# Two heads' float32 products of a gated recurrence take turns in the two row halves of the TensorE array

## The chip, the cores and the metric

The kernel runs on one core of one Trainium2 chip. The metric is the device time of one execution in microseconds (us); a smaller time is better. A kernel is timed in several executions, and the median is compared.

## What is computed

The reference is one layer of a diffusion backbone for 640 tokens of 1024 channels: 128 context tokens and 512 latent ones. One input projection feeds three branches (attention, a gated linear recurrence in both directions, a Fourier mixing); each is gated, and one output projection closes the layer. The change lies in the recurrence, cut here to one direction:

```python
def step(s, inp):                        # one chunk of 64 positions, 4 heads of 64 x 64
    qc, kc, vc, gc = inp
    G = jnp.cumsum(gc, axis=2)           # gc: log of the forget gates
    diff = G[:, :, :, None, :] - G[:, :, None, :, :]
    decay = jnp.exp(jnp.where(causal[:, :, None], diff, -jnp.inf))
    attn = jnp.einsum('bhtd,bhsd,bhtsd->bhts', qc, kc, decay)
    o = jnp.einsum('bhtd,bhde->bhte', qc * jnp.exp(G), s) + jnp.einsum('bhts,bhse->bhte', attn, vc)
    ...
    s_new = jnp.exp(G_last[:, :, 0, :])[..., None] * s + jnp.einsum(
        'bhsd,bhse->bhde', kc * jnp.exp(G_last - G), vc)
    return s_new, o
...
return o_f + flip(o_b), jnp.stack([s_f, s_b], axis=1)
```

## The kernel before, in words

**Tiles.** Channels lie on the 128 partitions, and the 640 tokens are five tiles of 128: tile 0 is the context, tiles 1 to 4 are latent. The recurrence has four heads of 64 channels, worked on as two pairs: pair p has one head on partitions 0 to 63 (`hh` = 0) and the other on 64 to 127 (`hh` = 1), so that a product of one head alone uses one row half of the TensorE array.

**Levels.** The products of queries and keys under their decays (`attn` above, both directions in one matrix) are built by `recurrence(p)` in seven levels, with block lengths 1, 2, 4 ... 64 (`LEVELS`, line 23). At a level, ScalarE copies the halves of the decayed queries and keys into `QB` and `KB` (lines 449 to 452); VectorE and GpSimd multiply the queries and keys by their gates for the next level (455 to 458), and VectorE multiplies the gates of neighbours (463, 464). Then `level` (432 to 439) forms, for each head, five float32 products of 64 x 128 by 64 x 128, one a token tile: four into one PSUM bank, the fifth (`i` = 4) into another. VectorE copies out of the bank those positions that belong to this level (`copy_predicated` with the mask of the level, line 439) into `AL` (four tiles of both heads, 128 x 512 each head) and `AC` (the fifth, 128 x 128 each). The seven masks and the diagonal (476, 477) cover every position once. The order is: head 0, four tiles; head 1, four tiles; head 0, last tile; head 1, last tile. The vector work of a level does not read the products of the level before it; the two meet only in the banks and the buffers.

**After the levels** keys are transposed by token, the states before each tile are formed (`kt`, `pst`, `sall`), and outputs are products of `AL`, `AC` with the values and of the decayed queries with the states.

**PSUM.** Five banks have the tag `b` (`WB["pb"]`), three the tag `f`. `PB()` takes the next of the five; the projections that run beside the recurrence accumulate in `f` banks.

**What sets the order.** Each part of the work is a generator; the class `Order` merges them, earlier streams first, by the estimates in `LAT` and by `od.now`, which `mm` (111 to 114) advances. The recurrences and the attention come ahead of `fill()`, which delivers the input projections one block after another (`zb0 qr0 zb1 qr1 ir0 P0 P1 ga0 ...`, P being the value, query and key blocks of an attention pair). The framework then schedules all of it again by a timeline of its own (`schedule_with_timeline_sim`; `IN_ORDER` is off), so the final order on each engine is fixed when the kernel is built, and each engine works through its list in order.

**Projections** are sums of three products of float32r parts (`mm3`): "W, hT" rows of 128 x 320 or, for `ir0`, 128 x 256. They are the work with which TensorE fills the time in which the levels' operands are made.

Of the kernel before, what the change touches and what calls it, by code (L numbers as in the profile page):

```python
# [17 lines left out]
P = 128  # L18
# [21 lines left out]
class Order:  # L40
    """Merges streams of statements into one: each is a generator that yields after a piece of TensorE work, with the
    time in us that its next piece has to wait for other engines, or the name of an event; earlier streams go first."""
# [30 lines left out]
def mixer_kernel(ctx: ExitStack, tc: tile.TileContext, A, O):  # L73
# [37 lines left out]
    def mm(out, lhsT, rhs, start=True, stop=True):  # L111
        n, m = rhs.free_size(), lhsT.free_size()
        od.now += 1e-3 * (n * 0.4167 * 4 if rhs.dtype == F32 else max(n * 0.4167, m * 0.83)) + 2e-3
        te.matmul(out, lhsT, rhs, start=start, stop=stop)  # L114
# [28 lines left out]
    # lower bounds of the forget gates: softmax and running sum over depth (one layer)  # L143
# [9 lines left out]
    def rsqrt_mean(ss, n):  # L153
        """ss -> 1/sqrt(ss/n + eps), in place."""
# [23 lines left out]
    def load_w(src, lo_eng=None, shape=(KT, P), tags=("raw", "hi", "lo")):  # L178
        """1024 weights a partition, in two parts"""
        return split_w(load_raw(src, tags[0], shape), lo_eng, shape, tags[1:])  # L180

    def load(t, src):
        """loads that follow the weights issued so far"""
# [3 lines left out]
    def mod_cols(out, w):  # L187
        """[4, 128]: rows 0,1 = c_hi (w_hi + w_lo), rows 2,3 = c_lo (w_hi + w_lo)."""
# [12 lines left out]
    def mm3(out, w, k, u, first, last):  # L201
        """out += w[:, k].T @ h[k][:, half u], in three passes over the parts."""
# [92 lines left out]
    def block(name, use, lo_eng=gp):  # L295
        """128 columns of the projection; use(z, u) gets one half of the tokens, z = [128 channels, 320 tokens] in PSUM."""
# [30 lines left out]
    def twice_silu(out, z):  # L327
        """2 silu(z) = z (1 + tanh(z / 2)): tanh is in the tables of exp and of the sigmoid"""
# [10 lines left out]
    def by_token(src):  # L339
        """[128 channels, 640 tokens] -> PSUM [128 tokens, token tile, 128 channels], the first four tiles and the last."""  # L340
# [5 lines left out]
    def token_blocks(name, use, tokens, lo_eng=gp):  # L346
        """256 columns of the projection by token; use(z, i0, n) gets token tiles i0 .. i0 + n - 1, z = [128 tokens, n, 256
        channels] in PSUM. tokens(t, i): tile i of the tokens."""
# [28 lines left out]
    # the mixed channels: a gate times its branch, put together by the later of the two  # L377
    mx, branch = [None] * 8, [None] * 8

    def mixed(j, gate=None, result=None):  # L380
        """result(out, gate): writes their product"""
# [30 lines left out]
    def recurrence(p):  # L412
# [9 lines left out]
        # [positions within the tile, head, tile, positions]: 4 latent tiles, and the context  # L422
# [6 lines left out]
        def level(KB, QB, mask):  # L429
            mk = late["masks"][:, mask, :].unsqueeze(1)  # L430
            for i0, i1 in ((0, 4), (4, 5)):
                for hh in range(2):
                    pa = PB()
                    w = (i1 - i0) * P
                    for i in range(i0, i1):
                        mm(pa[:, (i - i0) * P:(i - i0 + 1) * P], KB[RS[hh], i * P:(i + 1) * P],
                           QB[RS[hh], i * P:(i + 1) * P])
                    out = AL[:, hh] if i0 == 0 else AC[:, hh:hh + 1, :]
                    ve.copy_predicated(out, mk.to_broadcast([P, i1 - i0, P]), pa[:, :w].rearrange("p (a t) -> p a t", t=P))
# [27 lines left out]
        # equal positions: one scalar for each token and head  # L467
# [13 lines left out]
        # keys by token, for the state updates  # L481
# [9 lines left out]
        # states before each latent tile  # L491
# [25 lines left out]
        # outputs by token, norm over each head, gate  # L517
# [604 lines left out]
```

## Time and profile before

| | |
|---|---|
| three timed executions | 499.99, 504.39, 509.48 us; median 504.39 us |
| the profiled execution | span 495.5 us from its first to its last instruction; its time with what lies around the span is not listed |
| TensorE busy | 462.7 us of the span, 93% |
| VectorE, ScalarE, GpSimd busy | 342.9, 224.3 and 195.1 us |
| mean granted TensorE clock | 0.963 |
| HBM | 43.68 MB read, 3.28 MB written, 95 GB/s over the span |

Busy time of an engine is the union of its instructions' durations. Matmuls are pipelined: each float32 product here leaves two matmul records, whose durations overlap, so what a run of them costs is read from the start of its first record to the start of the record that follows the run. In a timeline row the columns are start, length (of the merged group), engine, line, operation, tile written and read, shape, count, and in brackets the idle time of the engine ahead of it with what ended it. A row of the stages' table has the stretch, its length, busy time and count of instructions of each engine, granted clock, DMA share and GB/s. PE is TensorE, PEld its weight loads, DVE VectorE, ACT ScalarE, POOL GpSimd.

### The profile page before, as it was taken

The numbers are of one execution on the slowest core, as the hardware profiler recorded it, in microseconds if no ns is written. First come the engines' busy times: TensorE is split into PE (matmuls) and PEld (weight loads), VectorE is DVE, ScalarE is ACT, GpSimd is POOL, SyncE is SP. The second block draws the span as 40 slices with busy tenths as digits, with TensorE's granted clock in tenths as the row PEclk, the third lists the DMA queues.
The fourth block names the chain that finished last, engine by engine and source line by source line (L and its number), as shares of the span: only waits on it lengthen the run. The fifth ranks groups of instructions, "written<-read, shape, count | busy, mean of one in ns | idle before, by whom it ended". The sixth has DMA issues, their size and how long they took to land.

```text
span 495.5 us, 8372 instructions
## 1 busy us (share of the span) xinstructions
PE 462.7 (93%) x3120; PEld 417.5 (84%) x3120; DVE 342.9 (69%) x787; ACT 224.3 (45%) x561; POOL 195.1 (39%) x160
## 2 busy tenths in 40 slices
PE   3698999979999999969999999989999999999995
PEld 3677999878899999959998889879898879878884
DVE  5997857999957655683569785679673769740264
ACT  6784453625330524422524465543544555630242
POOL 2576424778451466360444213337135124130000
PEclk9858999989999999978999999999999999999998
DMA  7955414110021113110320334223243111262032
GB/s 269 392 219 196 128 47 145 44 66 0 1 63 36 50 51 104 46 50 0 91 93 13 117 102 127 83 89 112 95 150 119 44 54 44 70 232 80 2 115 97
DMA packets 19512, 47.49 MB, mean 96 GB/s; under 512 B 3196, under 2 KB 6924, under 8 KB 19472
## 3 DMA queue, kind: packets, MB, share of 16 engines
q1 hardware_dynamic: 19376, 46.94, 27.9%
q8 instruction: 24, 0.39, 0.3%
q14 instruction: 16, 0.13, 0.1%
q0 software_dynamic: 96, 0.02, 0.1%
HBM read 43.68 MB, written 3.28 MB: 95 GB/s over the span
## 4 chain that ended last, share of the span: by engine, by line
PE 66%; DVE 16%; issue 6%; DMA 5%; ACT 4%; POOL 2%; SPq 1%; POOLq 0%; DVEq 0%; ACTq 0%
PE pb L114 61%; PE pb L118 4%; DVE lo L122 3%; ACT hi L121 2%; DMA txa<-x 1%; DVE tqd L604 1%; DVE s L672 1%; DMA raw<-win 1%; DMA vs<-wss 1%; DVE tqd L605 1%; DVE t L419 1%; DMA cf<-vc 1%; DMA cf<-kc 1%; DVE pe L674 1%; DVE m L464 1%
## 5 line engine op out<-in xcount | busy, mean ns | idle before, releaser
L114 PE MATMUL pb<-hT,hi 128*128 128x320 f32 x832 | 192.1, 317 | 0.0
L114 PEld LDWEIGHTS pb<-hT,hi 128*128 128x128 f32 x832 | 140.5, 191 | 2.6 <-issue 0.2
L114 PE MATMUL pb<-hT,lo 128*128 128x320 f32 x416 | 130.9, 315 | 0.0
L122 POOL TENSOR_TENSOR lo<-raw,hi 128x1024 fp32r<-128x1024 f32 x26 | 63.8, 2456 | 93.5 <-ACT hi L121 83.0
L114 PEld LDWEIGHTS pb<-hT,lo 128*128 128x128 f32 x416 | 79.2, 190 | 0.7
L121 ACT CAST hi<-raw 128x1024 fp32r<-128x1024 f32 x46 | 48.4, 1051 | 42.9 <-PE pb L114 26.7
L114 PE MATMUL pb<-t,t 64*128 64x128 f32 (+2 forms) x414 | 55.4, 305 | 3.8 <-ACT t L452 2.9
L114 PEld LDWEIGHTS pb<-t,t 64*128 64x128 f32 (+1 forms) x414 | 46.6, 197 | 9.2 <-ACT t L452 3.1
L121 ACT CAST pT<-pb 128x256 fp32r<-128x256 f32 x64 | 23.4, 373 | 57.3 <-PE pb L118 42.5
L122 DVE TENSOR_TENSOR lo<-raw,hi 128x1024 fp32r<-128x1024 f32 x20 | 28.2, 1411 | 14.2 <-ACT hi L121 13.9
L122 DVE TENSOR_TENSOR pT<-pb,pT 128x256 fp32r<-128x256 f32 x64 | 26.3, 415 | 16.1 <-ACT pT L121 15.9
L114 PE MATMUL pb<-hi,c 128*4 128x128 f32 x192 | 29.7, 241 | 6.5 <-ACT hi L121 6.5
L114 PE MATMUL pb<-hi,mh 128*128 128x512 f32 (+1 forms) x108 | 31.9, 376 | 1.0 <-POOL mh L122 1.0
L114 PE MATMUL pb<-lo,c 128*4 128x128 f32 x192 | 29.0, 241 | 3.5 <-DVE lo L122 3.2
L118 PE MATMUL pb<-ident,pe 128*128 128x128 f32 x136 | 22.5, 285 | 4.9 <-DVE pe L674 4.9
L666 DVE TENSOR_REDUCE s<-pb 128x1 f32<-128x256 f32 x32 | 13.4, 418 | 15.3 <-PE pb L114 15.0
L114 PEld LDWEIGHTS pb<-hi,mh 128*128 128x128 f32 x108 | 19.6, 188 | 5.0 <-POOL mh L122 1.4
L114 PEld LDWEIGHTS pb<-hi,c 128*4 128x4 f32 x192 | 17.8, 93 | 6.8 <-ACT hi L121 6.5
L114 PE MATMUL pb<-pT,mh 128*128 128x512 f32 (+1 forms) x102 | 22.8, 367 | 0.0
L118 PEld LDWEIGHTS pb<-ident,pe 128*128 128x128 f32 x136 | 16.6, 145 | 6.9 <-issue 4.5
L114 PEld LDWEIGHTS pb<-lo,c 128*4 128x4 f32 x192 | 17.8, 93 | 4.9 <-DVE lo L122 3.7
L672 DVE TENSOR_TENSOR s<-s 128x1 f32<-128x1 f32 x32 | 15.1, 471 | 9.8 <-ACT pe L671 9.5
(217 smaller groups left out, 934.2 us busy)
## 6 DMA issues: line engine op xcount, KB each, us to landing
raw<-win SPq DMA_DIRECT2D x29, 512.0 KB, 3.4
raw<-wg SPq DMA_DIRECT2D x8, 512.0 KB, 3.4
raw<-wout SPq DMA_DIRECT2D x8, 512.0 KB, 3.3
vs<-wss SPq DMA_DIRECT2D x6, 512.0 KB, 5.8
raw<-wss SPq DMA_DIRECT2D x5, 512.0 KB, 5.8
pT<-wss SPq DMA_DIRECT2D x5, 512.0 KB, 5.0
t<-x SPq DMA_DIRECT2D x10, 256.0 KB, 5.3
o_y<-t SPq DMA_DIRECT2D x9, 256.0 KB, 2.0
```

The source lines that it names most:

```text
L114: te.matmul(out, lhsT, rhs, start=start, stop=stop)
L118: last_tr[0] = te.transpose(out, src, ident).ins
L121: (sc.copy if hi_eng is None else hi_eng)(hi, src)
L122: (ve if lo_eng is None else lo_eng).tensor_sub(lo, src, hi.bitcast(F32))
L419: ve.scalar_tensor_tensor(qb, q, 0.5, Tb, op0=ALU.mult, op1=ALU.mult)
L464: ve.tensor_mul(Tb, b1, b2)
L604: ve.tensor_copy(qd[hh][r, :], q[r, :])
L605: ve.tensor_copy(qd[hh][o, :], q[r, :])
L666: ve.reduce_max(m[:, 0:1], pss[:, 256:512], axis=AX.X)
L672: ve.tensor_add(m[:, 2:3], m[:, 2:3], m[:, 3:4])
L674: NE.tensor_scalar(pe, pe, m[:, 2:3], 0.5, op0=ALU.mult, op1=ALU.mult)
```

## The change

In `level`, both heads get their bank first, and their products alternate tile by tile, head 1 ahead of head 0: (1, 0), (1, 0) ... The order within such a set is held by `follow`, which adds an ordering without a semaphore between each product and the one before it, so the later scheduling can put other work between them but not reorder them. `Order`'s clock is advanced by half of the products' estimate. At the first level (`li == 0`), ScalarE copies the whole bank into `AL` and `AC`, without a mask; the other six levels and the diagonal overwrite what isn't theirs. Comments and docstrings are removed too, which shifts line numbers (114 stays, 118 becomes 125, and so on).

```diff
     def mm(out, lhsT, rhs, start=True, stop=True):
         n, m = rhs.free_size(), lhsT.free_size()
         od.now += 1e-3 * (n * 0.4167 * 4 if rhs.dtype == F32 else max(n * 0.4167, m * 0.83)) + 2e-3
-        te.matmul(out, lhsT, rhs, start=start, stop=stop)
+        return te.matmul(out, lhsT, rhs, start=start, stop=stop).ins
+
+    def follow(chain, ins):
+
+        if chain:
+            tc.add_manual_dep(ins, chain[-1].name, mybir.DependencyInfo(mybir.DependencyClass.NoSync,
+                                                                        mybir.DependencyReason.DATA), reason="turns")
+        chain.append(ins)
...
-        def level(KB, QB, mask):
-            mk = late["masks"][:, mask, :].unsqueeze(1)
+        def level(KB, QB, li):
+
+
+            mk = late["masks"][:, li, :].unsqueeze(1)
             for i0, i1 in ((0, 4), (4, 5)):
+                pa = [PB(), PB()]
+                t, chain = od.now, []
+                for i in range(i0, i1):
+                    for hh in (1, 0):
+                        ins = mm(pa[hh][:, (i - i0) * P:(i - i0 + 1) * P], KB[RS[hh], i * P:(i + 1) * P],
+                                 QB[RS[hh], i * P:(i + 1) * P])
+                        follow(chain, ins)
+                od.now = 0.5 * (t + od.now)
                 for hh in range(2):
-                    pa = PB()
-                    w = (i1 - i0) * P
-                    for i in range(i0, i1):
-                        mm(pa[:, (i - i0) * P:(i - i0 + 1) * P], KB[RS[hh], i * P:(i + 1) * P],
-                           QB[RS[hh], i * P:(i + 1) * P])
                     out = AL[:, hh] if i0 == 0 else AC[:, hh:hh + 1, :]
-                    ve.copy_predicated(out, mk.to_broadcast([P, i1 - i0, P]), pa[:, :w].rearrange("p (a t) -> p a t", t=P))
+                    src = pa[hh][:, :(i1 - i0) * P].rearrange("p (a t) -> p a t", t=P)
+                    if li == 0:
+                        sc.copy(out, src)
+                    else:
+                        ve.copy_predicated(out, mk.to_broadcast([P, i1 - i0, P]), src)
```

**The second level on TensorE.** `pb_1100` is a projection; `pb_1107` and the other three are the banks of pair 0's second level. Before:

```order
L114 MATMUL pb_1100<-hT_107,hi_1068 128x320
L114 MATMUL pb_1100<-hT_108,hi_1068 128x320
L114 MATMUL pb_1100<-hT_107,lo_1069 128x320
L114 MATMUL pb_1107<-t_1054,t_1055 128x128 x4
L114 MATMUL pb_1113<-t_1054,t_1055 128x128 x4
L114 MATMUL pb_1119<-t_1054,t_1055 128x128
L114 MATMUL pb_1122<-t_1054,t_1055 128x128
```

Now:

```order
L114 MATMUL pb_1108<-t_1054,t_1055 128x128
L114 MATMUL pb_1100<-hT_107,hi_1068 128x320
L114 MATMUL pb_1100<-hT_108,hi_1068 128x320
L114 MATMUL pb_1100<-hT_107,lo_1069 128x320
L114 MATMUL pb_1100<-hT_107,hi_1068 128x320
L114 MATMUL pb_1100<-hT_108,hi_1068 128x320
L114 MATMUL pb_1107<-t_1054,t_1055 128x128
L114 MATMUL pb_1108<-t_1054,t_1055 128x128
```

The first product (head 1) stands alone, five projection products follow, and then the other nine alternate (seven more rows of them follow the last one shown). Over the fourteen levels the list has sixteen sets of level products in a row: fourteen with five products in the fuller half (one of these has a sixth), and two single ones; the profile before shows twenty-two. From the first level of pair 1 to the last level, 77 projection products of 128 x 256 stand between the levels both before and now, and 36 of 128 x 320 before against 103 now.

**The first level's copies.** VectorE before, between the gate work of the two pairs (`m`, `t`):

```order
L464 TENSOR_TENSOR m_1234<-t_980 128x320
L439 COPY_PREDICATED AL_991<-masks,pb_1036 128x512
L439 COPY_PREDICATED AL_991<-masks,pb_1042 128x512
L464 TENSOR_TENSOR m_1004<-m_1004 128x160
L439 COPY_PREDICATED AC_992<-masks,pb_1048 128x128
L439 COPY_PREDICATED AC_992<-masks,pb_1051 128x128
L330 SCALAR_TENSOR_TENSOR t_1097<-t_1097,pb_1072 128x320
```

ScalarE now; ahead of them a copy of the second level's keys, behind them the query block's tanh and the third level's copies:

```order
L468 COPY t_1055<-t_856 128x160x2
L453 COPY AL_991<-pb_1037 128x512
L453 COPY AL_991<-pb_1036 128x512
L453 COPY AC_992<-pb_1049 128x128
L453 COPY AC_992<-pb_1048 128x128
L336 ACTIVATE t_1097<-pb_1072 128x320
L465 COPY t_1125<-t_985 128x80x4
```

The four copies have left VectorE's list; the rest of it keeps its order there. Each pair does this once.

**In the attention, VectorE's list** moves too, by the new schedule. `tqd` are the queries of attention pair 1, `s_2252` and `s_2277` the sums of two softmax units of pair 0, `pe` their probabilities, which TensorE transposes. Before:

```order
L605 CAST tqd_2089<-tq_2088 64x640
L122 TENSOR_TENSOR pT_2241<-pb_2267,pT_2240 128x2x128
L604 CAST tqd_2090<-tq_2088 64x640
L605 CAST tqd_2090<-tq_2088 64x640
L672 TENSOR_TENSOR s_2252<-s_2252 128x1
L610 COPY tk_2081<-pb_2386 128x128
L612 COPY tk_2081<-pb_2386 128x4x48
L672 TENSOR_TENSOR s_2277<-s_2277 128x1
L673 RECIPROCAL s_2252<-s_2252 128x1
L673 RECIPROCAL s_2277<-s_2277 128x1
L674 TENSOR_SCALAR pe_2253<-pe_2253,s_2252 128x512
```

Now the four casts stand ahead of the whole softmax of these units:

```order
L620 CAST tqd_2089<-tq_2088 64x640
L621 CAST tqd_2089<-tq_2088 64x640
L620 CAST tqd_2090<-tq_2088 64x640
L621 CAST tqd_2090<-tq_2088 64x640
L129 TENSOR_TENSOR pT_2239<-pb_2242,pT_2238 128x2x128
L682 TENSOR_REDUCE s_2252<-pb_2251 128x1
```

On TensorE, 59 projection products stood between these units' scores and the transposes of the first of them; now 47 do.

## The prediction

> **What bounds the kernel now.** I read the page first: which engine has the span, and whether the chain that ended last runs through it.
>
> ```profile
> PE 462.7 (93%) x3120; PEld 417.5 (84%) x3120; DVE 342.9 (69%) x787; ACT 224.3 (45%) x561; POOL 195.1 (39%) x160
> PE 66%; DVE 16%; issue 6%; DMA 5%; ACT 4%; POOL 2%; SPq 1%; POOLq 0%; DVEq 0%; ACTq 0%
> ```
>
> TensorE is busy for 93% and is 66% of the chain. Next the table by stage, around the levels:
>
> ```profile
> 60.00:87.00 27.00, 27.00 (x186) 26.99 (x185) 17.90 (x23) 13.77 (x30) 9.91 (x9) 1.00 0.31 106
> 87.00:105.00 18.00, 17.19 (x138) 15.72 (x136) 17.24 (x27) 8.26 (x18) 14.25 (x12) 1.00 0.18 61
> 105.00:120.00 15.00, 12.18 (x78) 10.73 (x78) 14.94 (x29) 8.51 (x22) 11.08 (x12) 0.77 0.06 17
> 120.00:165.00 45.00, 45.00 (x371) 41.55 (x371) 33.81 (x88) 15.77 (x36) 20.04 (x26) 1.00 0.09 27
> ```
>
> Projections alone (60 to 87) go at 27.00 / 186 = 0.145 us each. The levels lie between 87 and 155. Up to 120, VectorE is as full as TensorE or fuller (17.24 of 18, 14.94 of 15); from 120 TensorE has no idle time at all and VectorE a quarter. So time taken from TensorE's list after 120 should move the end, and time taken before it only as far as VectorE follows. Then the levels themselves, in TensorE's timeline; the row behind a set gives its end, by starts:
>
> ```profile
> 87.40 1.93 PE L114 MATMUL pb<-t,t 64*128 64x128 f32 x20
> 89.26 0.42 PE L114 MATMUL pb<-hT,lo 128*128 128x320 f32 x1
> ...
> 91.36 1.16 PE L114 MATMUL pb<-t,t 64*128 64x128 f32 x8
> 93.09 1.16 PE L114 MATMUL pb<-t,t 64*128 64x128 f32 x10 [0.58 <-DVE AL L439]
> 94.40 0.48 PE L114 MATMUL pb<-t,t 64*128 64x128 f32 x2 [0.15 <-DVE AC L439]
> 94.81 0.56 PE L114 MATMUL pb<-hT,hi 128*128 128x320 f32 x2
> ...
> 99.08 1.93 PE L114 MATMUL pb<-t,t 64*128 64x128 f32 x20
> ...
> 107.82 4.54 PE L114 MATMUL pb<-t,t 64*128 64x128 f32 x28 [2.90 <-ACT t L452]
> 112.30 0.58 PE L114 MATMUL pb<-hi,hT 128*128 128x256 f32 x1
> ...
> 115.39 0.49 PE L114 MATMUL pb<-t,t 64*128 64x128 f32 x2
> 115.80 0.50 PE L114 MATMUL pb<-hi,hT 128*128 128x256 f32 x2
> ...
> 128.09 0.49 PE L114 MATMUL pb<-t,t 64*128 64x128 f32 x4
> 128.51 0.39 PE L114 MATMUL pb<-hi,hT 128*128 128x256 f32 x1
> ...
> 133.06 2.49 PE L114 MATMUL pb<-t,t 64*128 64x128 f32 x28
> 135.48 0.50 PE L114 MATMUL pb<-hi,hT 128*128 128x256 f32 x2
> 136.50 1.38 PE L114 MATMUL pb<-t,t 64*128 64x128 f32 x12
> 137.81 1.28 PE L114 MATMUL pb<-bones,t 128*128 128x2 f32 x10
> ```
>
> Two records are one product. A single one costs 115.80 - 115.39 = 0.41 us. Two of opposite heads side by side cost 128.51 - 128.09 = 0.42: the second is free. The twelve records from 136.50 are four products of head 1, one of head 0, one of head 1; five in one half, and 1.31 us. Hence in one half the first costs 0.41 and each further one (1.31 - 0.41) / 4 = 0.225, and the other half runs beside it when its products stand near enough. Today's order of four and four gets part of that: a level in one piece takes 89.26 - 87.40 = 1.86 us, where five and five wholly side by side would take 1.31.
>
> **The change, part by part.**
>
> *Turns.* All level products together, and the two kinds of copy that leave VectorE or come to ScalarE, as groups:
>
> ```profile
> L114 PE MATMUL pb<-t,t 64*128 64x128 f32 x280 | 32.9, 304 | 3.6 <-ACT t L452 2.9 <-DVE AL L439 0.6 <-DVE AC L439 0.2
> L439 DVE COPY_PREDICATED AL<-masks,pb 128x512 f32<-128x512 uint32 x28 | 20.0, 733 | 1.1 <-PE pb L114 1.0
> L439 DVE COPY_PREDICATED AC<-masks,pb 128x128 f32<-128x128 uint32 x28 | 7.1, 289 | 0.0
> L489 ACT COPY t<-pb 128x512 f32<-128x512 f32 x4 | 2.2, 588 | 1.2 <-PE pb L118 1.2
> ```
>
> The 280 records are busy for 32.9 us; taken from each set's first start to the next record's start, which leaves out tails under other work, the 22 sets hold 32.1. Before the stall at 107.82 stand three levels: 1.86, 94.81 - 91.36 = 3.45, and the third, from 99.08, with the records and the length of the first, 7.2 in all. Behind it stand 32.1 - 7.2 = 24.9 us for eleven levels.
>
> Now, by the new order of TensorE: ahead of the stall three sets of 1.31 and one single product of 0.42, 4.4 us. Behind it eleven sets, 14.4, one single, 0.4, one set with a sixth product, 0.2, and a surcharge for the clock, since the set behind the stall runs slowly: the same 28 records took 4.48 us there and 2.42 at 133.06, so my 1.5 us become 2.8, another 1.3. Together 16.3. Saved behind the stall: 24.9 - 16.3 = **8.6 us**. The bounds: 6.0 if only the whole-level difference of 0.55 counts, eleven times (the split sets of before then come back at other places); 9.9 if the surcharge goes.
>
> What stands behind a level product in TensorE's list are projections, and they move up. That the operands come in time is the point to check: the time is refilled by 103 - 36 = 67 more projections of 128 x 320 between the first level of pair 1 and the last, 67 x 0.145 = 9.7 us, against 8.6 saved. So the levels need not come faster from VectorE than they do now; that work leaves the time after the levels.
>
> *Ahead of the stall* TensorE would arrive 7.2 - 4.4 = 2.8 us sooner and wait longer for the copies of pair 1's first level (the bracket at 107.82). The chain that ended last shows what these wait for:
>
> ```profile
> 91.34 1.04 DVE m L464
> 92.39 0.66 DVE AL L439
> 93.05 0.04 issue
> 93.09 1.17 PE pb L114 x9
> 94.26 0.28 DVE AC L439
> 94.55 0.39 DVE t L330
> ```
>
> VectorE's queue, first-level copies among it. They leave it: 2 x 0.73 + 2 x 0.29 = 2.04 us. ScalarE, busy 8.26 of 18, takes them at 0.59 for 128 x 512 (a PSUM copy of that size; for the small one I take half, an estimate), and behind them wait the tanh of the query block and the third level's copies: the products end near 87.40 + 1.31 = 88.7, the four copies 1.8 later, 90.5, and VectorE takes up the tanh (L330) only at 94.55. I take most of what VectorE sheds, **1.8 us**. Bounds: 0 (ScalarE hands the delay back) and 2.8 (TensorE's own gain). In the second pair the same four copies leave VectorE too, off the path by then; without that cover they would be worth 2 us more.
>
> *The single product* split from its set costs 0.42 twice and is in the sum. `follow` adds no semaphore and no instruction. The 280 records and their weight loads stay as many.
>
> *Elsewhere the new schedule* moves rows in the attention. I book it at zero with both ends open; the largest place is the stall at 216:
>
> ```profile
> 208.30 1.91 DVE L605 CAST tqd<-tq 64x640 fp32r<-64x640 f32 x1
> ...
> 211.71 1.40 DVE L672 TENSOR_TENSOR s<-s 128x1 f32<-128x1 f32 x1
> ...
> 213.50 2.03 DVE L672 TENSOR_TENSOR s<-s 128x1 f32<-128x1 f32 x1
> ...
> 216.27 1.09 PE L118 MATMUL pb<-ident,pe 128*128 128x128 f32 x4 [3.87 <-DVE pe L674]
> ...
> 216.20:226.50 10.30, 10.23 (x36) 9.14 (x37) 5.54 (x20) 3.13 (x11) 3.31 (x2) 0.50 0.15 52
> ```
>
> TensorE waits 3.87 us, and then 10.3 us pass at half clock, 5.1 lost: 9.0 together. The casts leave that chain, but TensorE arrives 12 projections, 1.7 us, sooner. I take the stall as it is.
>
> **Sum.** 8.6 + 1.8 = 10.4 us. The profiled span of 495.5 becomes 485.1. The timed runs lie 4.5 to 14.0 above that span, the median 8.9; I carry the median over: 504.4 - 10.4 = **494.0 us**. By the bounds alone (6.0 to 12.7) 491.7 to 498.4.
>
> **Rivals.** *A, the stall at 216 goes too.* For it: four casts, one of 1.91 us, leave the way between the exponentials and the sums. Against: two 128 x 1 operations of 1.40 and 2.03 us stay in it. It gives 494.0 - 9.0 = 485.0. [...]
>
> *B, the levels are paced by VectorE.* Then what TensorE saves behind 107.82 comes back as waits at the level products, and only the 1.8 remain: 502.6. For it: 14.94 of 15 us up to 120. Against: 33.81 of 45 behind it, no wait of TensorE there, and the 9.7 us of projections moved in. [...]
>
> *C, two banks at once: slower.* A set now needs both heads' banks free before its second product, and all projections behind that product wait in TensorE's list. At level two before, such waits were 0.58 + 0.15. If each of eleven levels waits w, the loss is 11 w, and it decides from 10.4 / 11 = 0.95 us on; at 2 us it is 22 - 10.4 = 11.6 slower, 516. Against: the 77 and 103 projections between the eleven sets make 18 a gap, 18 x 0.145 = 2.6 us in which a bank can be emptied.
>
> *D, turns don't overlap.* If each change of half costs a fresh start, ten products take ten times 0.41: 14 x 4.1 - 32.1 = 25 us more, 529. Against: the pair at 128.09.
>
> **How the numbers follow.** Forecast 0.50, A 0.18, B 0.24, C 0.05, D 0.03. A measurement here tells about 2% (10.1 us) from no change, so the forecast, at 10.4, lies on that edge: 0.28 of its 0.50 count as faster, 0.22 as within. Faster 0.28 + 0.18 = 0.46; within 2% 0.22 + 0.24 = 0.46; slower 0.08. The range has A's time at its lower end and B's with a little of the spread of the runs at the upper: 484.5 to 504.
>
> **What would show it.** Right: whole sets of twenty records of about 1.31 us from start to next start, all level products busy near 20 us instead of 32.9; the wait ahead of pair 1's first level longer by about 1 us; no new wait at later level products; 24 `copy_predicated` into `AL` instead of 28. Wrong: sets of 1.9 or more (D), waits on `AL`, `AC` or the level copies after 110 (B, C), or a difference that stems from the attention (A).

## The result, and the profile after

The changed kernel took 486.31 us (median of four executions, 483.91 to 486.81) beside 506.94 us for the kernel before on the same chip (499.99, 504.39, 509.48 and 522.38). The ratio is 0.967, with a 95% interval from 0.958 to 0.977; it and the ratios below leave out executions in the slower state of the chip, here 509.48 and 522.38 us, and the plain medians would give 0.959. On a further chip (f1 below) it came out as 0.969 (0.962 to 0.976). The change makes the kernel faster by 2.3 to 4.2%. The forecast was 494.0 us, and the measured time lies inside its range of 484.5 to 504.0, near the end that belongs to rival A (485.0).

The profiled executions compare with less spread. First the page of the kernel after, its totals and its chain:

```profile
span 485.0 us, 8362 instructions
PE 451.8 (93%) x3120; PEld 406.0 (84%) x3120; DVE 342.2 (71%) x779; ACT 224.5 (46%) x569; POOL 197.5 (41%) x160
PE 59%; DVE 24%; ACT 8%; issue 4%; DMA 4%; POOL 0%; SPq 0%; DVEq 0%; ACTq 0%
```

The span went from 495.5 to 485.0 us. TensorE is busy 10.9 us less with the same 3120 matmul records, and the chain that ended last now runs through VectorE for 24% instead of 16%. Next the groups of the level products and of their copies:

```profile
L114 PE MATMUL pb<-t,t 64*128 64x128 f32 x280 | 22.8, 297 | 5.9 <-ACT t L468 3.2 <-DVE AL L455 2.6
L455 DVE COPY_PREDICATED AL<-masks,pb 128x512 f32<-128x512 uint32 x24 | 16.4, 736 | 11.8 <-PE pb L114 11.7
```

The products are busy for 22.8 us instead of 32.9. The idle time ahead of them is 5.9 us instead of 3.6, and what grew is the part that waits for VectorE's copies out of the banks: 2.6 for 0.6. The timeline of TensorE shows both (start, length, then as before; each set is followed by the row that gives its end):

```profile
87.49 1.39 PE L114 MATMUL pb<-t,t 64*128 64x128 f32 x20
88.81 0.41 PE L114 MATMUL pb<-hT,lo 128*128 128x320 f32 x1
...
97.09 0.49 PE L114 MATMUL pb<-t,t 64*128 64x128 f32 x2
98.11 1.82 PE L114 MATMUL pb<-t,t 64*128 64x128 f32 x18 [0.54 <-DVE AL L455]
99.87 0.50 PE L114 MATMUL pb<-hi,hT 128*128 128x256 f32 x2
...
107.05 2.60 PE L114 MATMUL pb<-t,t 64*128 64x128 f32 x22 [3.22 <-ACT t L468]
109.59 0.58 PE L114 MATMUL pb<-hi,hT 128*128 128x256 f32 x1
...
120.25 1.78 PE L114 MATMUL pb<-t,t 64*128 64x128 f32 x20 [2.02 <-DVE AL L455]
121.95 0.80 PE L114 MATMUL pb<-hi,hT 128*128 128x256 f32 x2
...
125.53 1.38 PE L114 MATMUL pb<-t,t 64*128 64x128 f32 x20
126.84 0.39 PE L114 MATMUL pb<-hi,hT 128*128 128x256 f32 x1
...
206.11 0.63 PE L125 MATMUL pb<-ident,pe 128*128 128x128 f32 x4
```

A whole set takes 126.84 - 125.53 = 1.31 us. The third set takes 99.87 - 97.09 = 2.78, because banks in its midst were not free (0.54 us of wait on `AL` at 98.11, 0.09 on `AC` at 99.45); at 120.25 TensorE waits 2.02 us for a bank, a wait that was not there before. The wait of 3.87 us ahead of the transposes at 216.27 is gone: the same transposes start at 206.11, with no bracket. Last the stages' table of the kernel after, at the places where the clock is low now or was low before:

```profile
107.40:110.90 3.50, 3.50 (x28) 3.28 (x25) 3.44 (x7) 2.08 (x6) 2.34 (x4) 0.51 0.03 7
121.10:124.50 3.40, 3.40 (x22) 3.18 (x20) 3.40 (x13) 1.54 (x4) 1.54 (x2) 0.50 0.02 5
206.00:216.00 10.00, 9.63 (x56) 7.94 (x55) 8.31 (x19) 4.31 (x15) 6.01 (x3) 1.00 0.15 52
295.20:302.00 6.80, 6.80 (x22) 5.17 (x22) 1.29 (x5) 2.23 (x8) 0.44 (x1) 0.50 0.05 19
```

The half clock behind the stall at 107 is shorter (3.4 us; before it went from 107.0 to 113.8), and the one at 216 is gone. There is a new one behind the wait at 120, and one at 295, where no wait of the 30 us ahead is longer than 0.63 us.

How far the kernel after leads can be read where both have just done the same work on TensorE, by the starts of the same projection product (counting the products of 128 x 320 and 128 x 256 from W and hT). The 600th stands in the projections ahead of the old stall; it starts at 211.06 before and at 203.42 after, 7.6 us sooner. The 660th stands behind the stall and starts 15.2 us sooner (236.03 and 220.88). At the end of the span 10.5 us are left. In f1 below these leads are 6.5, 14.0 and 9.2. The stretch with the stall was thus worth 7.5 us (7.5 to 7.6 in e1, e2, e7 and e8 below as well), as much as all that came ahead of it, and 4.7 were given back later. The half clock at 295 took 2.9 of these: e2 below has the same list on TensorE there and keeps its full clock (the mean of all its `pb<-tks,tqlo` rows of 64x256, some of which stand there, is 382 ns, 394 after), and gains 2.9 us on the kernel after in that place.

### The profile page after: what moved, and what is told of

It is laid out like the page before. It is cut to its first block, busy times and chain, and to the rows that moved or that the text cites. A ratio compares the mean times of both kernels' runs of the same rounds, so it can differ in the third digit from the quotient of the medians.

```text
span 485.0 us, 8362 instructions
## 1 busy us (share of the span) xinstructions
PE 451.8 (93%) x3120; PEld 406.0 (84%) x3120; DVE 342.2 (71%) x779; ACT 224.5 (46%) x569; POOL 197.5 (41%) x160
## 4 chain that ended last, share of the span: by engine, by line
PE 59%; DVE 24%; ACT 8%; issue 4%; DMA 4%; POOL 0%; SPq 0%; DVEq 0%; ACTq 0%
PE pb L114 55%; DVE lo L129 4%; PE pb L125 3%; ACT hi L128 3%; DMA vs<-wss 2%; DVE t L472 1%; DVE pT L129 1%; DVE tqd L620 1%; DVE t L471 1%; DMA cf<-vc 1%; DVE pe L690 1%; DVE t L426 1%; DVE m L480 1%; DVE tks L634 1%; DVE AL L455 1%
## 5 line engine op out<-in xcount | busy, mean ns | idle before, releaser
L114 PEld LDWEIGHTS pb<-hT,hi 128*128 128x128 f32 x832 | 138.9, 188 | 4.1 <-DVE row L129 0.6
L114 PEld LDWEIGHTS pb<-hT,lo 128*128 128x128 f32 x416 | 78.2, 188 | 1.1
L114 PE MATMUL pb<-t,t 64*128 64x128 f32 (+2 forms) x414 | 44.9, 300 | 7.8 <-ACT t L468 3.2
L114 PEld LDWEIGHTS pb<-t,t 64*128 64x128 f32 (+1 forms) x414 | 37.6, 195 | 12.6 <-DVE AL L455 3.6
L129 DVE TENSOR_TENSOR lo<-raw,hi 128x1024 fp32r<-128x1024 f32 x20 | 27.0, 1350 | 15.4 <-ACT hi L128 15.2
L129 DVE TENSOR_TENSOR pT<-pb,pT 128x256 fp32r<-128x256 f32 x64 | 26.3, 415 | 10.7 <-ACT pT L128 10.4
L686 ACT ACTIVATE pe<-pb,s 128x256 f32<-128x256 f32 x32 | 15.2, 474 | 21.6 <-DVE s L685 19.9
L455 DVE COPY_PREDICATED AL<-masks,pb 128x512 f32<-128x512 uint32 x24 | 16.4, 736 | 11.8 <-PE pb L114 11.7
L125 PE MATMUL pb<-ident,pe 128*128 128x128 f32 x136 | 21.5, 276 | 3.0 <-DVE pe L690 1.6
L114 PE MATMUL pb<-pT,mh 128*128 128x512 f32 (+1 forms) x102 | 22.5, 366 | 0.2 <-ACT pT L128 0.2
L688 DVE TENSOR_TENSOR s<-s 128x1 f32<-128x1 f32 x32 | 11.1, 347 | 14.8 <-ACT pe L687 14.5
```

The source lines that it names most:

```text
L114: return te.matmul(out, lhsT, rhs, start=start, stop=stop).ins
L125: last_tr[0] = te.transpose(out, src, ident).ins
L129: (ve if lo_eng is None else lo_eng).tensor_sub(lo, src, hi.bitcast(F32))
L455: ve.copy_predicated(out, mk.to_broadcast([P, i1 - i0, P]), src)
L686: sc.activation(pe[:, 256:512], pss[:, 256:512], ACT.Exp, bias=m[:, 1:2], accum_out=m[:, 3:4])
L688: ve.tensor_add(m[:, 2:3], m[:, 2:3], m[:, 3:4])
```

## The experiments

All spans below are those of the profiled execution, and "sets" is the time of the level products from the start of each set to the start of the row behind it, waits inside a set included. "Stall at 216" is the wait of 3.87 us with the half clock behind it.

| kernel | time, us (median, range) | span | sets | stall at 216 |
|---|---|---|---|---|
| before, timed four times over | 506.94; 517.35; 519.88; 507.21 | 495.5 | 32.1 | yes |
| after | 486.31 (483.91 to 486.81) | 485.0 | 22.3 | no |
| f1, after again | 484.95 (483.97 to 488.11) | 486.3 | 21.9 | no |
| e1, one row half | 496.14 (493.47 to 497.41) | 493.3 | 35.5 | no |
| e2, turns alone | 484.68 (483.09 to 485.34) | 482.9 | 22.0 | no |
| e3, ScalarE alone | 501.72 (498.61 to 504.95) | 496.8 | 30.4 | yes |
| e5, casts back | 481.71 (480.74 to 485.02) | 480.1 | 22.5 | no |
| e6, turns, order free | 495.60 (493.76 to 496.09) | 493.7 | 26.8 | yes |
| e7, copies first | 485.93 (484.36 to 487.00) | 483.6 | 22.7 | no |
| e8, key sums moved | 488.06 (486.31 to 489.36) | 484.5 | 24.9 | no |
| f2, turns and casts back | 482.43 (480.96 to 483.67) | 480.4 | 22.4 | no |
| f3, fixed, four and four | 497.01 (495.65 to 501.59) | 495.4 | 30.2 | yes |

The theory to be tested first: the gain comes from the overlap of the two row halves; the rival: it comes from the new schedule, the stall at 216 above all, or from ScalarE's copies.

### e1: the same order, but both heads in one row half

```diff
-                        ins = mm(pa[hh][:, ...], KB[RS[hh], i * P:(i + 1) * P],
-                                 QB[RS[hh], i * P:(i + 1) * P])
+                        ins = mm(pa[hh][:, ...], KB[RS[0], i * P:(i + 1) * P],
+                                 QB[RS[0], i * P:(i + 1) * P])
```

> The changed kernel with both heads' level products read from partitions 0 to 63 (the second head's products are thereby those of the first), so that all ten products of a level use one row half; every instruction and its order on every engine stay those of the changed kernel (span 485.0 us). Ten products in one half cost 0.41 + 9 x 0.225 = 2.43 us against 1.315 measured in turns, 14 x 1.12 = 15.6 us more of TensorE. Theory (the overlap of the halves is what the time comes from): of the 15.6 the three early levels (3.3) go into the wait of 3.2 us at 107 and up to 2 more into the wait at 120, so a span of 493 to 498 us. Rival (the gain is the new order in the attention, and the overlap only becomes waits for VectorE): a span of at most 488 us.

This is the cleanest comparison, since every engine's list is that of the kernel after. The values that it computes for the second head are not those asked for. TensorE's timeline:

```profile
107.58 3.88 PE L114 MATMUL pb<-t,t 64*128 64x128 f32 x22 [1.28 <-ACT t L468]
111.39 0.58 PE L114 MATMUL pb<-hi,hT 128*128 128x256 f32 x1
...
122.44 2.50 PE L114 MATMUL pb<-t,t 64*128 64x128 f32 x20
124.86 0.50 PE L114 MATMUL pb<-hi,hT 128*128 128x256 f32 x2
```

A set takes 124.86 - 122.44 = 2.42 us in one half, 1.31 in two: the ten products follow each other at about 0.225 us, and the overlap is all of the difference. The sets hold 13.2 us more. Behind the levels (at 165.03 after) the same product starts 9.7 us later; most of the other 3.5 us vanishes in waits that get shorter, 1.28 instead of 3.22 at 107, none at 120. The span is 8.3 us longer, because e1 keeps its full clock at 295 (`pb<-tks,tqlo` 381 ns on the mean; it has 3.4 us of half clock at 416 instead). That is the theory's reading.

### e2 and e3: the turns alone, ScalarE's first level alone

e2 is the kernel after with this edit; e3 is the kernel before with ScalarE's copies of the first level and nothing else.

```diff
-                    if li == 0:
-                        sc.copy(out, src)
-                    else:
-                        ve.copy_predicated(out, mk.to_broadcast([P, i1 - i0, P]), src)
+                    ve.copy_predicated(out, mk.to_broadcast([P, i1 - i0, P]), src)
```

> The changed kernel with the first level copied by VectorE under its mask, as before; turns stay. Theory: the copies of the first level are worth the 0.8 us by which the wait at 107 ends sooner, so a span of 485 to 487 us. Rival (ScalarE's copies, by relieving VectorE by 4.1 us in the stage where it is full, are half of the gain): 489 us or more.

> The kernel before with the first level copied whole by ScalarE, products in the old order. Its order is nearly that of before (42 of some 2600 rows of TensorE differ). Theory: 0.8 us at the wait at 107, the stall at 216 and its slow clock stay: a span of 493 to 496 us. Rival (ScalarE's part is half of the gain): 490 us or less.

The turns alone, with VectorE doing the first level, give all of it: the span is 482.9, 2.1 us below the kernel after and below the 485 to 487 us that the theory had. But that lead is the clock's. From 145 on TensorE's list is the same in both kernels, and until 295 e2 is 0.7 us behind the kernel after (and 0.4 ahead of f1); there only the kernel after and f1 fall to half clock (f1's mean of the `pb<-tks,tqlo` rows is 394 ns too). So behind the levels ScalarE's copies are worth less than the 1.1 us by which the kernel after and f1, with one list, differ. They do move the first level of pair 1 (it starts at 107.05 after, at 108.59 in e2), but little of these 1.5 us is left behind the levels. In the kernel before, too, they leave the span where it was (496.8 beside 495.5). The ratios to the kernel before, timed beside them, 0.951 (0.941 to 0.960) and 0.984 (0.972 to 0.997), are lower than the spans would have it, because the kernel before was between 505 and 521 us there.

### e4 and e5: the casts of the attention

The prediction put the stall at 216 down to four casts between the exponentials and the sums of two softmax units. e4 is the kernel before with these casts ordered behind the probabilities (`mark` is the second unit's `TENSOR_SCALAR` on `pe`); e5 is the kernel after with them ordered between the exponentials and the sums again (`mark` is the second unit's small `TENSOR_SCALAR` ahead of its exponentials):

```diff
+            if p == 1:
+                for c in casts:
+                    tc.add_manual_dep(c, mark[0].name, mybir.DependencyInfo(mybir.DependencyClass.NoSync,
+                                                                           mybir.DependencyReason.DATA), reason="casts")
```

> The kernel before, with one ordering added on VectorE: the four casts of attention pair 1's queries come after the probabilities of two softmax units of pair 0, instead of between their exponentials and their sums. 27 rows of TensorE differ. Theory (the stall at 216 and the half clock behind it come from these casts; 3.9 + 5.1 us): the stall falls below 1.5 us, the clock stays, span 486 to 489 us. Rival (the stall comes from the slow 128 x 1 sums, or returns at the next place that waits for the queries): 493 to 497 us.

> The changed kernel, with one ordering added on VectorE: the four casts of attention pair 1's queries stand between the exponentials and the sums of pair 0's two softmax units again, as in the kernel before. From there on the order differs (395 rows of TensorE, all of it in or behind that place). Theory (these casts make the stall of 3.9 us and the half clock behind it): a wait of 2 us or more at the transposes near 206 to 212, and a span of 488 to 493 us against 485.0. Rival (the slow sums, or TensorE's arrival time, make it): no wait over 1 us there, span 484 to 486.

In e4 the stall is gone: the longest wait near it is 0.38 us at 244.19, at full clock. So the stall needs the casts there, or something that moves with them: GpSimd's subtractions of the queries read the casts, and they too come later. The times don't settle what that is worth. Of its four executions (492.72, 498.76, 514.17 and 514.92) two are below all of those of the kernel before that were timed beside it, and in the profiled one the clock stayed at half from 110.1 to 168.1, so its span is of no use.

e5 shows that casts in that place are not enough. They are back between the exponentials and the sums, and the stall does not come back: two waits of 0.73 and 1.08 us remain, without a half clock, and the span is the shortest of all. It is not before's list to the row, though: before, the first cast (205.80) stands ahead of the second unit's `TENSOR_SCALAR` (208.13) and thus of its exponentials, and all four stand ahead of the first sum; in e5 two do. What remains is to read VectorE's rows beside GpSimd's. Before, GpSimd's timeline:

```profile
205.44 2.42 POOL L122 TENSOR_TENSOR lo<-raw,hi 128x1024 fp32r<-128x1024 f32 x1 [1.33 <-ACT hi L121]
208.29 1.57 POOL L606 TENSOR_TENSOR tqlo<-tq,tqd 64x640 fp32r<-64x640 f32 x1 [0.43 <-DVE s L669]
211.30 1.79 POOL L606 TENSOR_TENSOR tqlo<-tq,tqd 64x640 fp32r<-64x640 f32 x1 [1.44 <-DVE tqd L604]
213.17 2.34 POOL L122 TENSOR_TENSOR lo<-raw,hi 128x1024 fp32r<-128x1024 f32 x1
```

VectorE's rows of the same stretch that the prediction does not show:

```profile
205.80 2.41 DVE L604 CAST tqd<-tq 64x640 fp32r<-64x640 f32 x1 [0.69 <-ACT tq L599]
208.13 0.14 DVE L669 TENSOR_SCALAR s<-s 128x1 f32<-128x1 f32 x1
...
210.66 0.49 DVE L604 CAST tqd<-tq 64x640 fp32r<-64x640 f32 x1
...
213.23 0.34 DVE L612 COPY tk<-pb 128x192 f32<-128x192 f32 x1
```

The same cast takes 0.49 us when GpSimd rests and 2.41 when it starts 0.36 us behind a GpSimd subtraction. The four long rows of VectorE (the casts at 205.80 and 208.30, the sums at 211.71 and 213.50) end at 208.21, 210.21, 213.11 and 215.53; the four GpSimd rows end at 207.86, 209.86, 213.09 and 215.51. Each long row ends 0.02 or 0.35 us behind the GpSimd row beside which it started, and a sum of one number a partition takes 2.03 us beside GpSimd's subtraction of 1024. The copy at 213.23, which reads a bank of PSUM, takes 0.34 us; it started 0.06 us behind the start of a GpSimd row of 2.34 and ended 1.9 ahead of that row's end. GpSimd's timeline in e5:

```profile
201.58 1.81 POOL L624 TENSOR_TENSOR tqlo<-tq,tqd 64x640 fp32r<-64x640 f32 x1 [1.94 <-DVE tqd L622]
204.01 1.88 POOL L624 TENSOR_TENSOR tqlo<-tq,tqd 64x640 fp32r<-64x640 f32 x1 [0.62 <-DVE tqd L622]
205.97 2.40 POOL L129 TENSOR_TENSOR lo<-raw,hi 128x1024 fp32r<-128x1024 f32 x1
```

And VectorE's there:

```profile
200.97 0.47 DVE L622 CAST tqd<-tq 64x640 fp32r<-64x640 f32 x1
201.47 0.49 DVE L623 CAST tqd<-tq 64x640 fp32r<-64x640 f32 x1
201.99 1.42 DVE L696 TENSOR_TENSOR s<-s 128x1 f32<-128x1 f32 x1
203.44 0.49 DVE L622 CAST tqd<-tq 64x640 fp32r<-64x640 f32 x1
...
205.03 0.88 DVE L696 TENSOR_TENSOR s<-s 128x1 f32<-128x1 f32 x1
...
206.24 2.42 DVE L698 TENSOR_SCALAR pe<-pe,s 128x512 f32<-128x512 f32 x1
```

Again each long row ends with a GpSimd row: 203.41 beside 203.39, 205.91 beside 205.89, 208.66 beside 208.37. The same holds beyond these seven rows. Of the 64 sums of this kind in the traces of the kernels before and after, 15 took more than 0.3 us (0.43 to 2.19; the others 0.14 to 0.29), and every one of the 15 ends 0.01 to 0.02 us behind a GpSimd row. What holds VectorE up inside such a row was not shown.

What this makes of the stall is an estimate from the rows. From 205.80 on VectorE works without a pause until the probabilities. Its two long casts and two long sums take 6.4 us more than usual (0.49 and 0.16). The four casts together take 5.3. Either is more than the 3.87 us that TensorE waited, so taking away the casts, or GpSimd's rows beside them, would each have been enough. In e5 three rows are longer than usual, by 3.9 us in all, and TensorE waits 0.73 and 1.08. In the kernel after two of the casts are held up as well (2.29 and 1.76 us, from 195.76 and 198.59), but ahead of the softmax, and both sums take 0.15 to 0.16. So, by these rows, a stall forms when several of VectorE's operations, one after another on the way to TensorE, each meet a GpSimd operation.

### f4: two subtractions moved from GpSimd to VectorE

The reading was then put to a test in the kernel before:

```diff
-        yield from block(name, use)
+        yield from block(name, use, ve if name == "ga0" else gp)
...
-        yield from block(f"va{p}", use_v)
+        yield from block(f"va{p}", use_v, ve if p == 2 else gp)
```

> The kernel before, with the low parts of two weight blocks (gate block 0 and value block 2, 128x1024 each) subtracted on VectorE instead of GpSimd, so that GpSimd runs no such operation while VectorE casts pair 1's queries and forms the sums of two softmax units. VectorE gets two operations more. Theory (VectorE's operations on buffers stand while a GpSimd operation runs): the casts take 0.49 us each instead of 2.41 and 1.91 beside those two, the sums 0.16 unless a query subtraction still runs beside them, the stall at 216 shrinks below 1.5 us and brings no half clock, and the span is 487 to 493 us. Rival (the casts stand in the way of the sums by their own length and number): the casts still stand ahead of the sums, VectorE has about 2 us more to do there, the stall is 3 us or more, and the span 494 to 500 us.

Its profiled execution took 2009 us with TensorE's rows at more than three times their length (1060 ns a projection product for 315), so no time of it can be set beside the others. VectorE's and GpSimd's rows have their usual length in it. GpSimd's there:

```profile
1485.98 2.35 POOL L122 TENSOR_TENSOR lo<-raw,hi 128x1024 fp32r<-128x1024 f32 x1 [32.77 <-ACT hi L121]
1488.29 3.54 POOL L606 TENSOR_TENSOR tqlo<-tq,tqd 64x640 fp32r<-64x640 f32 x2
```

VectorE's beside them:

```profile
1486.40 2.28 DVE L604 CAST tqd<-tq 64x640 fp32r<-64x640 f32 x1
1488.72 1.72 DVE L605 CAST tqd<-tq 64x640 fp32r<-64x640 f32 x1
1490.46 1.39 DVE L672 TENSOR_TENSOR s<-s 128x1 f32<-128x1 f32 x1
```

With two subtractions moved (24 of 128 x 1024 are left on GpSimd, of 26), another one of the same size ran beside the casts, and two casts and one sum were held up as before. So in this execution the edit did not take away what it was to take away. The two quickest other executions took 498.85 and 498.96 us, spans of 497.1 and 497.2, beside 497.48 and 498.25 of the kernel before on the same chip; the third took 510.07. The 487 to 493 us that the theory expected did not come. Whether the stall stayed in these executions can't be told without their traces. That VectorE is held up beside GpSimd is thus read from rows that end together, and not shown by taking the GpSimd rows away.

### e6 and f3: turns without a fixed order, a fixed order without turns

e6 leaves the scheduling free to reorder the products:

```diff
-                        follow(chain, ins)
```

f3 keeps the fixed order, with the old sequence of products:

```diff
-                for i in range(i0, i1):
-                    for hh in (1, 0):
+                for hh in range(2):
+                    for i in range(i0, i1):
```

> The changed kernel without the fixed order: products are issued in turns, and the scheduling may split and reorder them. Its list has 20 sets instead of 16, several of them four and four again, and the rest of the order is close to that of the kernel before (149 rows of TensorE differ from it, 592 from the changed one). Theory (turns pay only where a set stays whole, and the stall at 216 belongs to before's order): level sets of 25 to 28 us in all against 22.3 and 32.1, the stall at 216 back, a span of 489 to 494 us. Rival (the fixing does nothing): 484 to 486.

> The changed kernel with the order of a level's products fixed, but in the old sequence (four or one of head 0, then as many of head 1), still two banks at once and ScalarE's first level. Theory (the gain is the overlap that the turns give): the sets hold 29 to 34 us as before instead of 22.3, and the span is 492 to 500 us. Rival (fixing the order, or asking for both banks at once, is what helps): a span of 488 us or less. Also open is whether the stall at 216 of the kernel before is in this list; it counts 9 us.

TensorE's rows at pair 1's first level and at the transposes, in e6:

```profile
107.62 4.20 PE L114 MATMUL pb<-t,t 64*128 64x128 f32 x28 [5.12 <-ACT t L467]
...
213.26 1.09 PE L125 MATMUL pb<-ident,pe 128*128 128x128 f32 x4 [3.87 <-DVE pe L689]
```

The same two places in f3:

```profile
108.15 4.54 PE L114 MATMUL pb<-t,t 64*128 64x128 f32 x28 [4.31 <-ACT t L468]
...
216.76 1.09 PE L125 MATMUL pb<-ident,pe 128*128 128x128 f32 x4 [3.87 <-DVE pe L690]
```

Without the fixed order the scheduling splits and reorders the products, and the sets hold 26.8 us instead of 22.3. With the fixed order and no turns they hold 30.2. Both kernels get a schedule close to the one before (from 178 on TensorE's list is the same), with the whole stall at 216 in it, and both are near it in time: f3's ratio is 0.994 (0.984 to 1.005). Just ahead of the stall e6 leads the kernel before by 3.0 us and f3 is 0.5 behind, where the kernel after leads by 7.6. So neither half of the edit gives the gain by itself. The change needs both, and its list happens to be one without the stall.

### e7 and e8: the waits at 120 and at 107

e7 orders VectorE's masked copies ahead of the gate work two levels later, so that the banks come free sooner:

```diff
+            for g in (ve.tensor_mul(qf2, qf2, bc(f1, h)).ins, ve.tensor_mul(qb1, qb1, bc(b2, h)).ins):
+                if li - 2 in copied:
+                    tc.add_manual_dep(g, copied[li - 2].name, ...)
```

e8 takes the sum of the keys off GpSimd's list ahead of the levels (it is formed with the gates, and multiplied by the queries at the fourth level):

```diff
-        gp.tensor_add(qk, kf, kb)
-        gp.tensor_mul(qk, qk, q)
...
+            if li == 3:
+                gp.tensor_mul(qk, qk, q)
```

> The changed kernel, with VectorE's list held so that the masked copies of a level come before the gate work of two levels later; 28 rows of TensorE's order and 30 of VectorE's differ. Theory (the wait of 2.0 us at 120 and the half clock behind it, 1.7 us, come from masked copies that stand in VectorE's list behind gate work of later levels): the wait at 120 goes, or falls under 0.5 us, sets near 21 us in all, span 481 to 484. Rival (VectorE is simply full there): the wait comes back at another level product within 10 us, span 484 to 486.

> The changed kernel, with GpSimd's two operations on the sum of both directions' keys moved: the addition to where the gates are made, the product with the queries behind the fourth level. They ran beside VectorE's first two products of pair 1 (1.69 and 2.16 us for 128 x 640, where the gate's 128 x 640 took 1.09). Theory (the wait at 107 is VectorE's chain, made long by GpSimd working beside it): those two products take 1.1 to 1.3 us each, the wait of 3.2 us falls by 1 to 1.5, span 482 to 484. Rival (something else is late there): the wait stays, span 485.

In e7 the wait at the third set is gone, the one at 120 has shrunk to 0.41 us (with another of 0.40 at 132), and that at 107 grows:

```profile
97.35 1.39 PE L114 MATMUL pb<-t,t 64*128 64x128 f32 x20
107.82 2.93 PE L114 MATMUL pb<-t,t 64*128 64x128 f32 x22 [5.19 <-ACT t L469]
...
119.00 1.38 PE L114 MATMUL pb<-t,t 64*128 64x128 f32 x18
120.79 0.49 PE L114 MATMUL pb<-t,t 64*128 64x128 f32 x2 [0.41 <-DVE AC L455]
```

The third set takes 1.31 us, and the 1.5 us reappear at 107, where TensorE now waits 5.19 us. Behind the levels e7 is 0.3 us ahead of the kernel after, so the time is about that of the kernel after. In e8 the wait at 107 vanishes, but TensorE waits inside the third set, which takes 5.67 us, and at 120 (3.08 us). Pair 1's first level starts at 108.97, later than in the kernel after. This does not refute e8's theory, for the edit did not clear GpSimd's list. VectorE's first product of pair 1 takes 0.82 us instead of 1.69, but the second still takes 2.18:

```profile
103.56 2.18 DVE L429 SCALAR_TENSOR_TENSOR t<-t,t 128x640 f32<-128x640 f32 x1
```

The schedule placed the moved multiplication beside it:

```profile
102.86 2.20 POOL L485 TENSOR_TENSOR t<-t,t 128x640 f32<-128x640 f32 x1 [1.36 <-DVE t L340]
```

In every kernel of the table this level starts between 106.9 and 109.0 us, whatever TensorE saved or lost ahead of it: up to there VectorE has the time (in the kernel after it is busy for 16.64 of the 18 us from 87 to 105).

### f1 and f2: again, and the quickest two edits together

f2 is e2 with e5's ordering of the casts.

> The changed kernel again, unedited, for its ratio to the kernel before on a further chip and beside the next kernel. It had 483.9 to 486.8 us, median 486.3. Expected: 483 to 488 us, span 482 to 485. The kernel before has had 500 to 525 us, so that a ratio between 0.93 and 0.98 comes out whichever of its executions are compared.

> Turns and fixed order, but the first level copied by VectorE with its mask, and the casts of attention pair 1's queries back between the exponentials and the sums: the two edits of the quickest kernels so far together. If each took away a cost of its own (2 us without ScalarE's copies, 4 us with the casts back), 480 to 483 us, 3 to 6 below the changed kernel in this call. Rival: both only drew other lists from the scheduling, and nothing adds up: 483 to 487 us, within 0.5% of the changed kernel.

On one chip f2 took 480.96 to 483.67 us, and the kernel after 483.97 to 488.11: no execution overlaps, and the medians stand 0.5% apart. The ratio to the kernel before is 0.964 (0.957 to 0.970). f2 has no half clock at 295, which both profiled executions of the kernel after have (0.50 in the table above); it has one of 3.4 us at 212.5. Whether f2 is better than e5, which kept ScalarE's copies and had 481.71 on another chip, the times don't tell. In f1 the wait at 120 is 3.30 us instead of 2.02, with 6.8 us of half clock, and the span is 1.3 us longer: so much can one execution of the same list differ.

## Why the prediction was right, and where it was not

**The price of a set** was right: 1.31 us forecast, 1.31 to 1.32 measured wherever a set runs at full clock without a wait inside. Rival D (25 us more, if turns didn't overlap) is out, and e1 shows that the overlap is the whole of the price: 2.42 us without it.

**The sum of the sets** was 20.7 us and came out as 22.3 (21.9 in f1). The difference is the third set, 2.78 instead of 1.31, and the one at 120.25, 1.71 at half clock instead of 1.31, less a surcharge for the clock at 107 that was put too high: the set there took 2.53, where 1.5 and 1.3 were booked.

**Behind the stall at 107, 8.6 us** was right in the sets and too much for the end. Ahead of the stall the sets hold 1.31 + 0.42 + 1.31 + 2.78 = 5.8 us, so behind it 22.3 - 5.8 = 16.5, where 16.3 were forecast. But a wait of 2.02 us at 120 and 1.7 us lost at half clock behind it, 3.7 together, went against the saving. The check that the operands would come in time (67 more projections, 9.7 us) counted the mean over 45 us. It missed that VectorE, which had 14.94 of 15 us up to 120, still owed the copies of the fourth level when TensorE came for the bank. This is rival B in a small form: it held up to 120 and not behind it, and it cost 3.7 us, not all of 8.6. What fills VectorE there is in part GpSimd again. Of its rows that start between 105 and 120 after, those longer than the shortest of the same operation and shape are longer by 6.5 us in all (3.8 before), and each ends behind a GpSimd row, 0.35 us for 128 x 320, 0.18 for 128 x 160, 0.05 for 128 x 20: a 128 x 320 product that meets one takes 0.91 to 1.22 us there instead of 0.48. No run took that away.

**Ahead of that stall, 1.8 us** was mis-sized: pair 1's first level starts 0.8 us sooner, and by e2 and e3 ScalarE's copies are worth less than the runs can tell. The two terms together were 10.4 us, and 7.6 were there ahead of the place of the old stall at 216 (6.5 in f1).

**The stall at 216, taken as staying,** was the step that failed. It went, as rival A said, with 0.18, and it was worth 7.5 us. The mechanism given for A is half of it. The casts did leave the way, and in e4 that is enough; but e5 has casts in the way and no stall, and by the rows it is GpSimd's operations beside VectorE's that make the casts and the sums long. The prediction quoted sums of 1.40 and 2.03 us against A as though they belonged there. The same operation takes 0.15 to 0.16 elsewhere, and a row that is ten times its usual length asks which engine ran beside it.

**What came from where.** Of the span's 10.5 us, the turns with their new order and ScalarE's copies gave 7.6 (6.5 in f1), the stall that went gave 7.5, and 4.7 were given back behind it, 2.9 of them at the half clock at 295. e1 agrees: with the same list and no overlap, the lead ahead of the old stall is not 7.6 but a lag of 2.0, so the overlap is worth 9.7 us at that place for 13.2 us of sets (against f1 8.5 for 13.6). These are readings of one or two profiled executions each. So the forecast of 485.1 us for the span met the 485.0 by luck: the level terms gave 2.8 us less than the 10.4, the stall gave 7.5 that were booked at nothing, and 4.7 that nobody had forecast were lost again.

**The median carried over** was wrong by itself. Each time lies 1.8 us above its own span, in both kernels; the profiled execution of before was one of its quickest (497.48 to 525.34 us over all executions, at granted clocks from 0.905 to 0.962), and the kernel after varies by 1% at 0.97 to 0.98. The 8.9 us between the median and the profiled span were the spread of the kernel before, and the kernel after doesn't have it. With 1.8 in their place the forecast would have been 486.9. Why the kernel before loses its clock in more of its executions is not settled here.

**C** (two banks at once make it slower) was to decide from 0.95 us a level on. The waits for a bank behind the stall at 107 came to 2.02 us, 0.2 a level.

## What to carry to other kernels

Products of 64 rows that alternate between the two row halves cost here little more than half of what they do in one half (ten of them 1.31 us and 2.42), but only with the alternation fixed against the scheduling (all sets 22.3 us, without it 26.8). What TensorE saved ahead of a point that VectorE paced came back as a wait there (3.22 us at 107, where e1, whose ten products take 2.42 us, waited 1.28), so sum the savings behind such a point alone. To split a gain between causes, compare the starts of one and the same product at places where both kernels have done the same work; the ends of the spans hide what came and went between. Before an edit is blamed or thanked for a stall, compare each row in the chain with the same operation elsewhere: where one is several times too long, see which engine ran beside it and whether the two end together. Any new schedule may remove or make such a meeting, so look in the trace whether an edit did take it away. Put the forecast against the profiled span, and look at the spread of the timed executions before a difference between median and span is carried over.

## What the runs showed of the hardware

The two halves overlap nearly perfectly: ten products of 64x128x128 in float32 take 1.31 us in turns, as five in one half did at 136.50 before; they take 1.86 in the order of four and four, and 2.42 in one half. An operation of VectorE that met one of GpSimd took up to 14 times its usual length (a sum at 375.37 after, 2.19 us for 0.16; it ends 0.02 us behind the GpSimd row).

In the traces of the kernels before and after half clock came in stretches of 3.4 us or small multiples, the end of the span apart, where no product is left: 13.7, 3.4, 6.8 and 10.2 us before (from 21.6, 45.5, 107.0 and 216.2), 13.7, 3.4, 3.4 and 6.8 after (from 22.1, 107.4, 121.1 and 295.2). All but the one at 295.2 began within a wait of TensorE of 1.57 to 3.87 us, or less than 2 us behind one. The length of the wait alone did not decide: 2.02 us at 120.25 after were followed by half clock, 3.20 us at 107 in f1 were not. The same two waits at the transposes were followed by it in f2 (0.73 and 1.10 us) and not in e5 (0.73 and 1.08). In the profiled execution of e4 it lasted 58 us, with TensorE busy for 57.40 of them (stages' table, columns as before):

```profile
110.10:168.10 58.00, 57.40 (x258) 49.94 (x256) 30.56 (x76) 15.72 (x39) 17.84 (x21) 0.50 0.03 10
```

These 58 us are seventeen times 3.4, and no run tells why the clock stayed at half so long.
